# Gate products with the gate-scaled one-hot as the stationary operand and the plain one-hot streamed

## The chip, the core and the metric

The kernel runs as one program on one core of a Trainium2 chip. Its engines are TensorE (PE; PEld is its weight load), VectorE (DVE), ScalarE (ACT), GpSimd (POOL) and SyncE (SP, which here only issues transfers). The metric is the device time of one execution in microseconds; lower is better. The kernel before takes 2062.15 us, the median of three runs (2058.58 to 2062.66).

## What is computed

Two decoder layers over 256 tokens of 1024 channels, in float32. Each has a mixer (layer 0: mLSTM heads beside block-sparse attention; layer 1: differential attention) and then a PEER channel mixer, which is where the change lies. PEER looks up 128 of 16384 experts for each token: 8 heads, 16 experts each. The reference, cut to that:

```
qry = (xt @ wq).reshape(t, 8, 2, 128)
sub = einsum('thpd,pnd->thpn', qry, keys)            # 2 x 128 sub-keys
s_top, i_top = top_k(sub, 16)
cand_s = s_top[:, :, 0, :, None] + s_top[:, :, 1, None, :]
cand_i = i_top[:, :, 0, :, None] * 128 + i_top[:, :, 1, None, :]
score, pos = top_k(cand_s, 16); idx = cand_i at pos
gate = softmax(score)
act = gelu(einsum('td,thkd->thk', xb, u[idx])) * gate
out = einsum('thk,thkd->td', act, v[idx])
```

An expert's number is 128 i + j, with i from the first half of the keys and j from the second.

## The kernel before

The kernel gathers nothing. It computes all 16384 activations for all 256 tokens, multiplies them by a gate that is zero nearly everywhere, and multiplies by all of v. Products stand in float32 precision by two parts: every weight tile of 128x1024 is loaded by SP (`load`, L149) into a ring, copied by ScalarE to a rounded part hi (L159), and VectorE forms the rest lo (L162). TensorE then runs three products for each of the eight channel blocks (L185 hi by hi, L186, L187), each with 128x128 stationary weights and 256 moving tokens.

PEER (`peer_body`) has four stages for each layer:

- 16 query tiles and the scores; VectorE starts on the top-16 searches.
- The first tiles of u (`h_tile`, one tile of 128 experts, all j of one i): A[:, i, :] = gelu(u_i . h), while VectorE finishes the searches. They leave three tables with the 128 slots (16 x 8 heads) on partitions and the tokens along the free axis: "i" and "g" (the gate, scaled by 32768, in two fp16 parts) and "jn", the negative of j.
- The gate stretch: the other tiles of u up to 128, and between them 64 gate groups of four tokens each (`G_TOK`), spread evenly up to tile 120. Most tiles have a group behind them, about every fourth has none.
- 128 tiles of v (L920 to L922), with A as the activations.

The gate of token t for expert (i, j) is the sum over the slots k of g_k (j_k = j)(i_k = i). That is a product of two one-hot matrices over the 128 slots. `gate_onehots` makes them for four tokens: oj, the one-hot of j, a dense block of 128 values of j for each token (by ScalarE with five activations in five of eight groups, L1068 and L1069, else by VectorE, L1072); oi, the one-hot of i with the four tokens innermost (VectorE, L1078), and og, that times either part of the gate (L1081, twice). `gate_group` then runs eight products (L1094: four tokens by two parts) with 128 slots as the contraction, oj as the stationary operand and og[:, w, :, k] as the moving one; they add up in PSUM to [j, 4 tokens, i]. Below the tile at which the stretch stands, VectorE multiplies A by them (L1101); above, ScalarE writes them into A (L1103), and a later `h_tile` multiplies by gelu (L950).

The order is that of the Python code, per engine, after a scheduler that may move an instruction on its own engine. The one-hots of group n + 1 are asked for ahead of the products of group n. og and the dense one-hot have two buffers, the plain token-innermost one has one; PSUM tiles "h" and "g" have two banks each. On TensorE a group stands whole between the 24 products of one tile and those of the next.

Of the kernel before, what the change touches and what calls it, by code (L numbers as in the profile page):

```python
# [20 lines left out]
P = 128  # L21
# [34 lines left out]
class Cols:  # L56
    """Column offsets of the packed per-partition constants."""
# [17 lines left out]
class Prog:  # L75
# [8 lines left out]
    # ---------------------------------------------------------------- setup  # L84
# [52 lines left out]
    def psum(self, tag):  # L137
        """One PSUM bank: h, g in every phase; l, t in the mixers and acc in the PEER."""
        pool, bufs = (self.ps, 2) if tag in "hg" else (self.ps2, {"l": 2, "t": 2, "acc": 4}[tag])
        return pool.tile([P, 512], F32, tag=tag, name=f"ps_{tag}", bufs=bufs)  # L140
# [4 lines left out]
    # ------------------------------------------------------------- weights  # L145
# [6 lines left out]
    def split(self, raw, late=None):  # L152
        """A tile as the sum of two that products take in one pass; from late on, the parts are left to norm_apply."""
# [20 lines left out]
    def mm_col(self, pss, ws, act, kds=range(KD)):  # L174
        """pss[i][128, 256] = ws[i]^T @ act over 1024 rows; both operands in two parts."""
# [13 lines left out]
    def col_tiles(self, aps, act, tags, kds=range(KD), ws=None, rest=None):  # L189
        """Products of the first few tiles, channel block by channel block as act's blocks come in; then one by one."""  # L190
# [11 lines left out]
    def take(self, ap):  # L202
        """The split tile of ap; the splits of the tiles that follow in self.feed go out ahead of need."""
        if not self.feed and not self.ready:
            return self.wsplit(ap)
        while self.feed and len(self.ready) <= AHEAD:
            self.ready.append(self.wsplit(self.feed.pop(0)))
        return self.ready.pop(0)

    def first_tiles(self, aps, late):  # L210
        """The first three tiles of a phase, loaded into the ring that outlives the phases."""
# [14 lines left out]
    def mm_row(self, pss, aps, act):  # L226
        """pss[tt][128 tokens, 512] = act^T @ w, w in four tiles of 2 x 128 rows."""
# [15 lines left out]
    # --------------------------------------------------------------- adaLN  # L243
    def ada(self, layer, cb, kds=range(KD)):
        """mod columns of block cb: (silu(c) @ ada_w + ada_b), channels on partitions."""
# [13 lines left out]
    # ---------------------------------------------------------------- norms  # L259
    def rsqrt(self, out, v):  # L260
        """out = v ** -0.5 for positive v, elementwise on a small tile."""
        self.nc.gpsimd.tensor_tensor(out=out, in0=v, in1=self.mhalf[:, :v.shape[-1]], op=ALU.pow)

    def keep_warm(self, n):
        """Products without a use while the norm's short chain runs: an idle tensor engine halves its clock."""
# [5 lines left out]
    def norm_stat(self, kd, warm=WARM):  # L271
        """Adds the squares of channel block kd; after the last, sums over channels, tokens on partitions."""
# [37 lines left out]
    def norm_apply(self, layer, which, r, t, hhi, hlo, kds=range(KD)):  # L310
        """h = x * rstd * (gain (1 + scale)) + shift in two parts; t holds the unshifted blocks."""
# [19 lines left out]
    def alibi(self, pool):  # L331
        """Distances from a query to the keys before it, without bound for the keys behind it."""
# [12 lines left out]
    # ------------------------------------------------- attention primitives  # L345
# [8 lines left out]
    def qk_norm(self, pool, zs):  # L354
        """RMS norm over each 64 channels of a q tile and a k tile; q also takes the logits' scale."""
# [29 lines left out]
    def softmax(self, pool, lg, q, k, h, qt, bias):  # L385
        """exp(logits - max) and its sum; q [64, 256], k [64, 256] of one head."""
# [12 lines left out]
    def transpose_p(self, pool, p0, p1):  # L399
        """P of both query tiles -> [keys 0..127, 256 queries], [keys 128..255, queries 128..255]."""  # L400
# [17 lines left out]
    # ------------------------------------------------------------- mixer 0  # L418
# [105 lines left out]
    def moba_pair(self, pool, hp, zs, bv, bias, yhi, ylo):  # L524
        """One pair of heads, in stages."""
# [32 lines left out]
    def advance(queue):  # L558
        """Takes each head in flight one stage further, the oldest first."""
# [4 lines left out]
    def mlstm_gates(self, pool, gp, out):  # L564
        """Row quantities of the mLSTM, one head per partition, time along the free axis."""
# [39 lines left out]
    def mlstm(self, pool, rows, qk, mv, mo, yhi, ylo):  # L605
# [12 lines left out]
        # state after the first chunk, its normaliser as column 128  # L618
# [21 lines left out]
        # num and, as column 128, den, tokens on partitions  # L640
# [34 lines left out]
        # h = num / max(|den|, exp(-m)); rms_norm(h) folds into one factor per token  # L675
# [30 lines left out]
    # ------------------------------------------------------------- mixer 1  # L706
    def mixer1(self):
# [3 lines left out]
        with ExitStack() as st:  # L711
# [28 lines left out]
            for i, ps in self.col_tiles(cols, h, ("h", "h", "l"), ws=ws):  # L740
# [6 lines left out]
                if i == 3:  # L747
                    # lambda, on every partition
# [18 lines left out]
    def diff_head(self, pool, hd, zs, v, vhave, bias, lam, og, yhi, ylo):  # L767
        """One head, in stages."""
# [44 lines left out]
    # ---------------------------------------------------------------- PEER  # L813
# [5 lines left out]
    def peer_body(self, layer, side, st):  # L819
# [7 lines left out]
        tabs = {"i": tab.tile([P, T], F16, name="it"), "jn": tab.tile([P, T], F32, name="jn"),  # L827
# [103 lines left out]
    def ffn_out(self, layer, kd, y):  # L931
        """x += gate * y for one block of channels."""
# [8 lines left out]
    def h_tile(self, ap, h, A, i, done=0):  # L941
        """A[:, i, :] = gelu(u_i . h), times the gates of the tokens below done, which A holds."""
# [11 lines left out]
    def scores(self, pool, subs, q, keys):  # L954
        """Products of one half head's queries with its sub-keys, tokens on partitions."""
# [24 lines left out]
    def top_k(self, sp, vals, idxs, tabs):  # L980
        """Top 16 of the 16 x 16 sums per head: expert rows i, columns j and gates, slots on partitions."""
# [8 lines left out]
        for tt in range(TT):  # L990
# [15 lines left out]
            # softmax gates  # L1006
# [10 lines left out]
            # position -> (a, b): 4 x 16 candidates, then 12 x 4  # L1017
# [13 lines left out]
            # b = (pos & 3) + (pos < 64) * (pos & 12),  pos & 3 = pos - 4 * (pos >> 2)  # L1031
# [23 lines left out]
            nc.vector.tensor_copy(tabs["i"][:, t], ps[:, 0:P])  # L1055
            nc.vector.tensor_scalar_mul(tabs["jn"][:, t], ps[:, P:2 * P], -1.0)
# [146 lines left out]
```

## Time and profile before

| what | value |
|---|---|
| median of the runs | 2062.15 us |
| span of the profiled execution | 2059.4 us (the page gives no other time for it) |
| TensorE busy | 2020.4 us, 98% |
| VectorE busy | 1536.9 us, 75% |
| ScalarE busy | 1136.4 us, 55% |
| moved by DMA | 376.84 MB, 183 GB/s on average |
| gate products (L1094) | 1024, 138.8 us busy with overlap |

Times in the rows are microseconds unless marked ns. A busy TensorE says little by itself: products overlap in the record, so one that follows another at 0.12 us has a duration of 0.28 us. What a product costs is read from start to start. PE and PEld rows count the same 16281 products and their loads.

### The profile page before, as it was taken

The numbers are of one execution on the slowest core, as the hardware profiler recorded it, in microseconds if no ns is written. First come the engines' busy times: TensorE is split into PE (matmuls) and PEld (weight loads), VectorE is DVE, ScalarE is ACT, GpSimd is POOL, SyncE is SP. The second block draws the span as 40 slices with busy tenths as digits, with TensorE's granted clock in tenths as the row PEclk, the third lists the DMA queues.
The fourth block names the chain that finished last, engine by engine and source line by source line (L and its number), as shares of the span: only waits on it lengthen the run. The fifth ranks groups of instructions, "written<-read, shape, count | busy, mean of one in ns | idle before, by whom it ended". The sixth has DMA issues, their size and how long they took to land.

```text
span 2059.4 us, 41035 instructions
## 1 busy us (share of the span) xinstructions
PE 2020.4 (98%) x16281; PEld 1963.3 (95%) x16281; DVE 1536.9 (75%) x3328; ACT 1136.4 (55%) x2129; POOL 48.3 (2%) x37
## 2 busy tenths in 40 slices
PE   5999999999999999999999999999999999999999
PEld 4888999999999999999988799999999999999999
DVE  8978998787897565677578789977788965556654
ACT  4655546777665444444455654667767644444443
POOL 0010000000000000000022100000000000000000
PEclk9999999999999999999999999999999999999999
DMA  8863355444444566898266143544444455559660
GB/s 329 293 192 131 114 185 177 144 152 146 142 152 159 200 211 202 329 321 301 91 226 204 52 159 121 185 165 152 145 146 150 145 167 183 184 186 343 217 192 25
DMA packets 104016, 376.84 MB, mean 183 GB/s; under 512 B 11536, under 2 KB 12944, under 8 KB 103696
## 3 DMA queue, kind: packets, MB, share of 16 engines
q1 hardware_dynamic: 103824, 374.22, 53.6%
q8 instruction: 128, 2.10, 0.4%
q14 instruction: 64, 0.52, 0.1%
HBM read 373.12 MB, written 1.05 MB: 182 GB/s over the span
## 4 chain that ended last, share of the span: by engine, by line
PE 88%; issue 5%; DVE 5%; ACT 1%; POOL 1%; DMA 0%; POOLq 0%; ACTq 0%; DVEq 0%
PE ps_h L185 13%; PE ps_h L187 13%; PE ps_h L186 13%; PE ps_acc L921 9%; PE ps_acc L922 9%; PE ps_acc L920 9%; PE ps_g L1094 6%; PE ps_h L922 3%; PE ps_h L921 3%; PE ps_h L920 3%; DVE lo L162 1%; PE ps_l L389 1%; PE ps_h L237 1%; PE ps_h L238 1%; PE ps_h L239 1%
## 5 line engine op out<-in xcount | busy, mean ns | idle before, releaser
L159 ACT CAST hi<-raw 128x1024 fp32r<-128x1024 f32 x613 | 640.6, 1046 | 730.6 <-PE ps_h L921 385.9
L162 DVE TENSOR_TENSOR lo<-raw,hi 128x1024 fp32r<-128x1024 f32 x613 | 748.7, 1221 | 346.4 <-ACT hi L159 342.8
L185 PE MATMUL ps_h<-h2hi,hi 128*128 128x256 f32 x2256 | 653.0, 289 | 0.4 <-ACT A L952 0.4
L186 PE MATMUL ps_h<-h2lo,hi 128*128 128x256 f32 x2256 | 638.4, 283 | 0.0
L187 PE MATMUL ps_h<-h2hi,lo 128*128 128x256 f32 x2256 | 638.2, 283 | 0.0
L185 PEld LDWEIGHTS ps_h<-h2hi,hi 128*128 128x128 f32 x2256 | 434.2, 192 | 1.2 <-ACT A L952 0.9
L920 PE MATMUL ps_acc<-act,hi 128*128 128x256 f32 x1536 | 434.4, 283 | 0.7 <-ACT act L904 0.7
L921 PE MATMUL ps_acc<-act,hi 128*128 128x256 f32 x1536 | 434.4, 283 | 0.1
L922 PE MATMUL ps_acc<-act,lo 128*128 128x256 f32 x1536 | 433.9, 283 | 0.0
L186 PEld LDWEIGHTS ps_h<-h2lo,hi 128*128 128x128 f32 x2256 | 433.0, 192 | 0.0
L187 PEld LDWEIGHTS ps_h<-h2hi,lo 128*128 128x128 f32 x2256 | 432.2, 192 | 0.7
L920 PEld LDWEIGHTS ps_acc<-act,hi 128*128 128x128 f32 x1536 | 294.5, 192 | 2.0 <-ACT act L904 1.7
L921 PEld LDWEIGHTS ps_acc<-act,hi 128*128 128x128 f32 x1536 | 294.8, 192 | 0.5 <-DVE act L905 0.5
L922 PEld LDWEIGHTS ps_acc<-act,lo 128*128 128x128 f32 x1536 | 294.7, 192 | 0.0
L1101 DVE SCALAR_TENSOR_TENSOR A<-A,ps_g 128x256 f32<-128x256 f32 (+28 forms) x214 | 124.5, 582 | 45.1 <-PE ps_g L1094 41.8
L921 PE MATMUL ps_h<-act,hi 128*128 128x256 f32 x512 | 144.8, 283 | 0.0
L922 PE MATMUL ps_h<-act,lo 128*128 128x256 f32 x512 | 144.8, 283 | 0.0
L920 PE MATMUL ps_h<-act,hi 128*128 128x256 f32 x512 | 144.6, 283 | 0.0
L1094 PE MATMUL ps_g<-og,oj 128*128 128x128 f16 x1024 | 138.8, 292 | 0.0
L252 DVE CUSTOM_DVE_ANT_0 raw<-raw,crow,small 128x1024 f32<-128x1024 f32 x96 | 122.6, 1279 | 18.3 <-DMA raw<-in_ada_w_dram 18.0
L1103 ACT ACTIVATE A<-ps_g 128x256 f32<-128x256 f32 (+39 forms) x170 | 69.4, 447 | 95.7 <-DVE A L1101 90.2
L1081 DVE TENSOR_TENSOR og<-oi,gt 128x512 f16<-128x512 f16 x256 | 100.9, 420 | 25.2 <-PE ps_g L1094 25.2
(319 smaller groups left out, 2654.7 us busy)
## 6 DMA issues: line engine op xcount, KB each, us to landing
raw<-in_uT_dram SPq DMA_DIRECT2D x256, 512.0 KB, 3.3
raw<-in_v_dram SPq DMA_DIRECT2D x256, 512.0 KB, 4.3
raw<-in_ada_w_dram SPq DMA_DIRECT2D x96, 512.0 KB, 4.6
raw<-in_wq_dram SPq DMA_DIRECT2D x32, 512.0 KB, 4.4
raw<-in_ev_in_dram SPq DMA_DIRECT2D x21, 512.0 KB, 5.1
raw<-in_od_in_dram SPq DMA_DIRECT2D x16, 512.0 KB, 4.4
raw<-in_ev_v_dram SPq DMA_DIRECT2D x8, 512.0 KB, 4.8
raw<-in_ev_out_dram SPq DMA_DIRECT2D x8, 512.0 KB, 4.1
```

Source lines behind the costliest of these rows:

```text
L159: nc.scalar.copy(hi, raw)
L162: self.last_lo = nc.vector.tensor_tensor(out=lo, in0=raw, in1=hi.bitcast(F32), op=ALU.subtract)
L185: nc.tensor.matmul(ps, lhsT=whi[:, s], rhs=ahi[:, kd, :], start=kd == kds[0], stop=False)
L186: nc.tensor.matmul(ps, lhsT=whi[:, s], rhs=alo[:, kd, :], start=False, stop=False)
L187: nc.tensor.matmul(ps, lhsT=wlo[:, s], rhs=ahi[:, kd, :], start=False, stop=kd == kds[-1])
L252: nc.vector.tensor_tensor_reduce(w, w, self.crow, 1.0, self.small[:, ab:ab + 1], ALU.mult, ALU.add, m)
L920: nc.tensor.matmul(acc[dt], lhsT=vhi[:, s], rhs=xhi, start=False, stop=False)
L921: nc.tensor.matmul(acc[dt], lhsT=vhi[:, s], rhs=xlo, start=False, stop=False)
L922: nc.tensor.matmul(acc[dt], lhsT=vlo[:, s], rhs=xhi, start=False, stop=m == NEXP - 1 and dt not in (0, 2))
L1081: nc.vector.tensor_tensor(out=og[:, w], in0=oi, in1=tabs["g"][:, w, ts].unsqueeze(1).to_broadcast(full), op=ALU.mult)
L1094: nc.tensor.matmul(pv[:, k, :], lhsT=oj[:, k, :], rhs=og[:, w, :, k], start=w == 0, stop=w == 1)
L1101: nc.vector.scalar_tensor_tensor(dst, dst, 1.0 / GSC, pv[:, :, lo:m], op0=ALU.mult, op1=ALU.mult)
```

## The change

The roles of the two one-hots are exchanged. The token-innermost one, which carries the gates, now stands for j (oj and og), and og[:, w, :, k] becomes the stationary operand. The dense plain one stands for i (oi) and is the moving operand. The output in PSUM is the same [j, token, i]. The tables follow: "in" is the negative of i in float32, "j" is j in fp16. Cut to the core:

```
-        tabs = {"i": tab.tile([P, T], F16, name="it"), "jn": tab.tile([P, T], F32, name="jn"),
+        tabs = {"in": tab.tile([P, T], F32, name="in"), "j": tab.tile([P, T], F16, name="jt"),
                 "g": tab.tile([P, 2, T], F16, name="gt")}
...
-            nc.vector.tensor_copy(tabs["i"][:, t], ps[:, 0:P])
-            nc.vector.tensor_scalar_mul(tabs["jn"][:, t], ps[:, P:2 * P], -1.0)
+            nc.vector.tensor_scalar_mul(tabs["in"][:, t], ps[:, 0:P], -1.0)
+            nc.vector.tensor_copy(tabs["j"][:, t], ps[:, P:2 * P])
...
     def gate_onehots(self, oh, tabs, t0):
         nc = self.nc
         ts = slice(t0, t0 + G_TOK)
-        oj = oh.tile([P, G_TOK, P], F16, tag="oj", name="oj")
+        oi = oh.tile([P, G_TOK, P], F16, tag="oi", name="oi")
         if self.ngate % 8 < J_ACT:
             for k in range(G_TOK):
-                nc.scalar.activation(oj[:, k, :], self.iota, AF.Square, bias=tabs["jn"][:, t0 + k:t0 + k + 1])
-            nc.scalar.activation(oj, oj, AF.Relu, scale=-1.0, bias=1.0)
+                nc.scalar.activation(oi[:, k, :], self.iota, AF.Square, bias=tabs["in"][:, t0 + k:t0 + k + 1])
+            nc.scalar.activation(oi, oi, AF.Relu, scale=-1.0, bias=1.0)
         else:
             for k in range(G_TOK):
-                nc.vector.tensor_scalar(oj[:, k, :], self.iota, tabs["jn"][:, t0 + k:t0 + k + 1], 0.0, op0=ALU.add,
+                nc.vector.tensor_scalar(oi[:, k, :], self.iota, tabs["in"][:, t0 + k:t0 + k + 1], 0.0, op0=ALU.add,
                                         op1=ALU.is_equal)
         self.ngate += 1
-        oi = oh.tile([P, NEXP, G_TOK], F16, tag="oi", name="oi", bufs=1)
-        og = oh.tile([P, 2, NEXP, G_TOK], F16, tag="og", name="og")
-        full = [P, NEXP, G_TOK]
-        nc.vector.tensor_tensor(out=oi, in0=self.iota4, in1=tabs["i"][:, ts].unsqueeze(1).to_broadcast(full),
+        oj = oh.tile([P, P, G_TOK], F16, tag="oj", name="oj", bufs=1)
+        og = oh.tile([P, 2, P, G_TOK], F16, tag="og", name="og")
+        full = [P, P, G_TOK]
+        nc.vector.tensor_tensor(out=oj, in0=self.iota4, in1=tabs["j"][:, ts].unsqueeze(1).to_broadcast(full),
                                 op=ALU.is_equal)
         for w in range(2):
-            nc.vector.tensor_tensor(out=og[:, w], in0=oi, in1=tabs["g"][:, w, ts].unsqueeze(1).to_broadcast(full),
+            nc.vector.tensor_tensor(out=og[:, w], in0=oj, in1=tabs["g"][:, w, ts].unsqueeze(1).to_broadcast(full),
                                     op=ALU.mult)
-        return oj, og
+        return oi, og
 
     def gate_group(self, ohs, A, t0, i_mul):
         nc = self.nc
         ts = slice(t0, t0 + G_TOK)
-        oj, og = ohs
+        oi, og = ohs
         pv = self.psum("g").rearrange("p (t i) -> p t i", t=G_TOK)
         for k in range(G_TOK):
             for w in range(2):
-                nc.tensor.matmul(pv[:, k, :], lhsT=oj[:, k, :], rhs=og[:, w, :, k], start=w == 0, stop=w == 1)
+                nc.tensor.matmul(pv[:, k, :], lhsT=og[:, w, :, k], rhs=oi[:, k, :], start=w == 0, stop=w == 1)
```

On TensorE, at the first gate groups of layer 0, these are the rows before, each load above its product (semaphores that a row waits for in brackets):

```order
L187 MATMUL ps_h<-h2hi,lo 128x256
L1094 LDWEIGHTS oj [waits DVE_49,Activation_49]
L1094 MATMUL ps_g<-og,oj 128x128 [waits PE_49]
L1094 LDWEIGHTS oj
L1094 MATMUL ps_g<-og,oj 128x128 [waits DVE_49]
L1094 LDWEIGHTS oj
L1094 MATMUL ps_g<-og,oj 128x128
```

And the same place now, where oi is the plain one-hot and og the one with the gates:

```order
L187 MATMUL ps_h<-h2hi,lo 128x256
L1094 LDWEIGHTS og [waits PE_49,DVE_49]
L1094 MATMUL ps_g<-oi,og 128x128 [waits Activation_49]
L1094 LDWEIGHTS og [waits DVE_49]
L1094 MATMUL ps_g<-oi,og 128x128
L1094 LDWEIGHTS og
L1094 MATMUL ps_g<-oi,og 128x128
```

No row moved; the loads now read og and wait for VectorE, which makes it, and the products read the plain one-hot. Before, the two products of a token had the same weights; now each has its own.

On VectorE, the piece of the difference at the first gate groups of layer 0 (A is named by its number, it and jt are the fp16 tables):

```order
-L1081 TENSOR_TENSOR og<-oi,gt 128x512 x2
+L1081 TENSOR_TENSOR og<-oj,gt 128x512 x2
 L162 TENSOR_TENSOR lo<-raw,hi 128x1024
 L1101 SCALAR_TENSOR_TENSOR A_2063<-A_2063,ps_g 128x4x38
-L1078 TENSOR_TENSOR oi<-iota_91,it 128x512
-L1081 TENSOR_TENSOR og<-oi,gt 128x512 x2
+L1078 TENSOR_TENSOR oj<-iota_91,jt 128x512
+L1081 TENSOR_TENSOR og<-oj,gt 128x512 x2
 L950 TENSOR_TENSOR A_2063<-A_2063,gelu 128x4
 L162 TENSOR_TENSOR lo<-raw,hi 128x1024
```

The shapes and the order are the same as before; only the names of the operands differ.

## Rows read from the trace of the kernel before

**Rows 1.** The page, its span, two engines, and the granted clock in 40 slices.

```profile
span 2059.4 us, 41035 instructions
...
PE 2020.4 (98%) x16281; PEld 1963.3 (95%) x16281; DVE 1536.9 (75%) x3328; ACT 1136.4 (55%) x2129; POOL 48.3 (2%) x37
...
PEclk9999999999999999999999999999999999999999
...
GB/s 329 293 192 131 114 185 177 144 152 146 142 152 159 200 211 202 329 321 301 91 226 204 52 159 121 185 165 152 145 146 150 145 167 183 184 186 343 217 192 25
```

**Rows 2.** The page, the chain that ended last: shares of the span by line.

```profile
PE ps_h L185 13%; PE ps_h L187 13%; PE ps_h L186 13%; PE ps_acc L921 9%; PE ps_acc L922 9%; PE ps_acc L920 9%; PE ps_g L1094 6%; PE ps_h L922 3%; PE ps_h L921 3%; PE ps_h L920 3%; DVE lo L162 1%; PE ps_l L389 1%; PE ps_h L237 1%; PE ps_h L238 1%; PE ps_h L239 1%
```

**Rows 3.** Timeline of TensorE around one gate group: start, us, engine, line, operands, count.

```profile
606.97 0.28 PE L187 MATMUL ps_h<-h2hi,lo 128*128 128x256 f32 x1
607.09 1.08 PE L1094 MATMUL ps_g<-og,oj 128*128 128x128 f16 x8
607.93 0.37 PE L185 MATMUL ps_h<-h2hi,hi 128*128 128x256 f32 x1
608.13 0.28 PE L186 MATMUL ps_h<-h2lo,hi 128*128 128x256 f32 x1
```

**Rows 4.** All instructions of line 1094: duration ns min/median/max, first and last start us.

```profile
L1094 PEld LDWEIGHTS <-oj x1024: 96/115/118, 355.8 to 1658.5; 128*128 128x128 f16 x171
L1094 PE MATMUL ps_g<-og,oj x1024: 274/294/296, 355.8 to 1658.7; 128*128 128x128 f16 x171
```

**Rows 5.** Float32 weight loads of 4, 64 and 128 columns: lines 372, 551, 363.

```profile
L372 PEld LDWEIGHTS ps_g<-ident,qr x24: 81/83/85, 104.8 to 1154.7; 128*4 128x4 f32 x24
...
L551 PEld LDWEIGHTS ps_t<-pT,bv x16: 137/137/137, 141.0 to 164.6; 128*64 128x64 f32 x16
...
L363 PEld LDWEIGHTS ps_g<-ind,qsq x96: 186/192/224, 94.8 to 1147.7; 128*128 128x128 f32 x96
```

**Rows 6.** All instructions of line 268, products of dense fp16 columns without a use.

```profile
L268 PEld LDWEIGHTS <-zero x24: 95/97/181, 185.1 to 1198.8; 128*128 128x128 f16 x24
L268 PE MATMUL ps_h<-iota,zero x24: 376/379/392, 185.2 to 1199.0; 128*128 128x512 f16 x24
```

**Rows 7.** Timeline of TensorE where three of line 268 follow each other.

```profile
185.15 0.82 PE L268 MATMUL ps_h<-iota,zero 128*128 128x512 f16 x3
```

**Rows 8.** Timeline of the weight loads of four products with two moving columns.

```profile
94.78 0.52 PEld L363 LDWEIGHTS ps_g<-ind,qsq 128*128 128x128 f32 x4
```

**Rows 9.** Gate stage stretches: length, PE, PEld, DVE, ACT, POOL busy, clock, DMA, GB/s.

```profile
355.00:400.00 45.00, 45.00 (x381) 44.52 (x380) 32.74 (x77) 35.48 (x91) 0.00 (x0) 1.00 0.42 142
...
600.00:640.00 40.00, 40.00 (x338) 39.60 (x338) 37.64 (x80) 26.18 (x67) 0.00 (x0) 1.00 0.45 147
```

**Rows 10.** Timeline of VectorE late in layer 0, one round with a gate group.

```profile
626.29 0.75 DVE L1101 SCALAR_TENSOR_TENSOR A<-A,ps_g 128x256 f32<-128x256 f32 x1 [1.07 <-PE ps_g L1094]
626.96 0.41 DVE L1081 TENSOR_TENSOR og<-oi,gt 128x512 f16<-128x512 f16 x1
627.29 0.39 DVE L950 TENSOR_TENSOR A<-A,gelu 128x232 f32<-128x232 f32 x1
627.60 0.58 DVE L1101 SCALAR_TENSOR_TENSOR A<-A,ps_g 128x196 f32<-128x196 f32 x1
628.10 0.41 DVE L1081 TENSOR_TENSOR og<-oi,gt 128x512 f16<-128x512 f16 x1
628.43 1.21 DVE L162 TENSOR_TENSOR lo<-raw,hi 128x1024 fp32r<-128x1024 f32 x1
629.57 0.41 DVE L1078 TENSOR_TENSOR oi<-iota,it 128x512 f16<-128x512 f16 x1
```

**Rows 11.** All instructions of line 1072, VectorE's way to the dense one-hot.

```profile
L1072 DVE TENSOR_SCALAR oj<-iota,jn x192: 235/252/292, 368.8 to 1653.4; 128x128 f16<-128x128 f16 x192
```

**Rows 12.** Waits in layer 0's gate stage: who waited for whom, us, times, longest.

```profile
DVE A L1101 <- PE ps_g L1094: 19.7, 28, 1.4
DVE og L1081 <- PE ps_g L1094: 12.6, 12, 1.5
```

## Prediction

> **What bounds the kernel now.** I read the page first: the span is 2059.4 us, TensorE is busy for 98% of it, and its granted clock stands at 9 tenths or more, which is its upper level of 2.4 GHz, in all 40 slices [rows 1]. So the clock is no lever, and what counts is how TensorE's time is filled. The chain of waits comes next: six entries for the big products, and at 6% the gate products of line 1094 [rows 2]. Nothing of VectorE but a few splits is on it. So an edit of the gate products changes the span one for one, as long as no other engine takes over.
>
> The timeline of TensorE shows what a gate group costs [rows 3]. From the start of L187 at 606.97 to the start of L186 at 608.13 are 1.16 us, with a group of eight between. Products of one tile follow at 0.12 us, so L187 to the L186 behind it is 0.24 us without a group. The group costs 0.92 us, 115 ns for each product. There are 1024 products [rows 4], so 128 groups and 118 us, close to the chain's 6% (124 us, rounded).
>
> What sets the 115 ns? A product has a load of 128 stationary columns and a stream of 128 moving ones. The load: float32 loads last 83 ns for 4 columns, 137 for 64 and 192 for 128 [rows 5], so about 80 ns that all have and 0.87 ns for a column. The fp16 load of the gate product lasts 96 ns when nothing holds it up (its minimum; 118 at most) [rows 4]. That leaves some 16 ns for the columns themselves, far less than 115. The stream: the products without a use of line 268 move 512 fp16 columns that lie densely. Three of them take 0.82 us with 0.38 for the last [rows 6, 7], so they follow at 0.22 us, 55 ns for 128 columns. Their duration says it again: at 0.43 ns a column, 384 columns fewer would shorten 379 ns to 214, and the gate product's shortest is 274 [rows 4, 6], 60 ns more. Its moving operand is og[:, w, :, k], every fourth fp16. So I read the 115 ns as a stream at half rate (110) and 5 ns of turnover; the load is hidden.
>
> **The change, part by part.** The number, shape and type of all instructions stay. The two one-hots trade places: the moving one (oi) is now dense, and the stationary one (og) is read with a step of four elements.
>
> *The stream.* 128 dense columns at line 268's rate take 55 ns instead of 110. This is the term on which all rests.
>
> *The load.* No row shows a strided stationary operand. From below: it costs what the dense fp16 load costs, 16 ns behind the fixed part, hidden behind 55 ns of stream; the pace is then 55 plus the 5 of turnover, 60 ns. From above: it falls back to the float32 load's pace, which is (0.52 - 0.19) / 3 = 110 ns where only two columns are streamed [rows 8], or even takes twice that, as the stream does now (220). I take the doubling of the fast load, 16 to 32 ns, since the same step doubles the stream; that still fits behind 55, and I leave 5 ns more for it in the open: 65 ns. The Trainium skill says in "TensorE: Matmul & The Clock Gate" (Weight-path perf modes) that the fast load applies to 128 weights that are not FP32, in four chunks packed or strided. By that the slow bound would not arise; the 96 ns against 192 agree on the type, and no run here shows the step. The same page (Back-to-back issue gap) gives about 81 ns as the sustained pace of load and product at 128 columns; as an estimate from it, a group would take 7 x 81 + 110 = 677 ns, save 243, and the time would be some 31 us under before's.
>
> *The last product of a group.* Behind it the float32 weights of L185 must be loaded, 110 ns, and only 65 ns of stream stand before them. So the eighth slot stays at 110. The group takes 7 x 65 + 110 = 565 ns instead of 920; it saves 355 ns, and 128 groups save 45 us.
>
> *VectorE and ScalarE.* Their instructions only trade operands: the table that is negated is now that of i, a 128x128 copy against a 128x128 scaling, twice per layer: nothing. But they have less time. In the gate stretches TensorE waits for nobody; VectorE is busy for 32.7 of 45 us early and 37.6 of 40 late [rows 9], because the part of A that it multiplies grows. Late in the layer, a round with a group takes 0.75 + 0.41 + 0.39 + 0.58 + 0.41 + 1.21 + 0.41 = 4.16 us of VectorE durations [rows 10]; neighbours overlap by some 0.08 us, so 3.6 us, and in 3 of 8 groups VectorE also makes the dense one-hot, four times 0.25 us [rows 11], 0.7 net of overlap. A round on TensorE shrinks from 3.80 to 2.88 + 0.57 = 3.45 us, but every fourth tile has no group, which gives VectorE its slack: over four tiles TensorE needs 4 x 2.88 + 3 x 0.565 = 13.2 us and VectorE about 3 x 3.6 + 1.6 + 0.8 = 13.2. So it is even only at the end of each layer, in the last 40 us or so of 285; before, VectorE has room. Its waits for the gate products (19.7 and 12.6 us in layer 0) [rows 12] are slack that it gives up first. I charge 3 us for both layers together; between 0 and 15 is possible. ScalarE has 26 to 35 us of work in 40 to 45 [rows 9]: covered. The weights arrive at 142 to 147 GB/s there [rows 9] and would have to come 9% faster; the first twentieth of the span moves twice that [rows 1].
>
> **Sum.** 2059.4 - 45 + 3 = 2017 us by the profiled span. The page gives no other time for that execution; the median of the runs shown, 2062.15, is 2.7 above, and I add 2.
>
> **Rivals.**
> *The load is half hidden.* The strided load steals reads from the stream or is turned over later, pace 80 to 105. A group then takes 670 to 845 ns and saves 250 to 75: 32 to 10 us, 2030 to 2052. For it: load and stream of a product both read SBUF, and the step has never been measured here. Against: float32 loads of 110 ns hide behind 120 ns products throughout.
> *VectorE becomes the bound.* If it cannot be filled beyond the 94% of the late windows [rows 9], the last 90 of 285 us of a layer shrink not at all: a third of the gain goes, 45 x 2/3 = 30, so 2032. Against: where VectorE idles late, it mostly waits for the gate product itself [rows 12].
> *Nothing changes.* Either the strided load falls to 110 ns, so 8 x 110 = 880 ns a group and 5 us won, or something else than the stream paces the products at 115, and the time stays at 2062. In this kernel the second would be a turnover per product that doesn't depend on the operands' step. Against it: pairs with float32 weights turn over at 110 ns [rows 8], so 115 is no floor of a pair. The Trainium skill, "SBUF — State Buffer" (Door 1: The DMA port swizzle), has a rule that speaks for it: access is at full rate as long as two elements fall into one 16-byte line, so up to 8 bf16 apart. By that rule a step of four is free now and there is nothing to win in the stream; the 60 ns that the gate product is too long speak against it.
> *Slower.* The strided stationary operand loses the fast path and pays double for the step as well: 220 ns, which nothing hides. A group then takes 8 x 220 = 1760 ns, 840 more: +107 us, 2169. It decides from a load of 115 ns on; at 130 it would be +15 us. For it: the stream pays just that today. Against: the load would have to become more than seven times as long as its 16 ns.
>
> **How the numbers follow.** Forecast (pace 55 to 80) 0.62; VectorE bound 0.12; half hidden 0.10; nothing changes 0.09; slower 0.07. The predicted time is 2019 us. Its own range is 2008 to 2032: the low end is a pace of 60 with nothing lost to VectorE (7 x 60 + 110 = 530, 390 saved, 50 us) and a little more. The range with the rivals goes up to 2050, which leaves out the last two cases and a few hundredths below. Faster by over 0.2% (about 4 us, what can be told from no change) 0.84, within 0.09, slower 0.07.
>
> **What would show it.** The start of L187 to that of L186 across a group should fall from 1.16 to about 0.81 us; the 128 groups should leave the chain with some 3 to 4% instead of 6. The fp16 load should show about 110 ns unhindered, not 190: that is the step on which I could be wrong. TensorE should stay without idle time in the gate stretches until their last 40 us, where a wait of L187 for the split of line 162, or of the gate product for og, may appear. I am wrong if the pace stays at 110 or more, or if TensorE's idle time takes back over 15 us.

## The result, and the profile after

The kernel after the change takes 2011.34 us (median of four runs, 2009.66 to 2012.62), against 2061.49 us for four runs of the kernel before (2058.58 to 2062.66): a ratio of 0.9756, 95% interval 0.9743 to 0.977. The forecast was 2019 us with a range of 2008 to 2050. The direction and the mechanism came out as argued; the gain is 50 us where 43 were forecast.

The page after, with the lines that answer to [rows 1, 2], and two of its groups (instructions, then busy us, mean ns of one, idle time of the engine before them and what ended it):

```profile
span 2010.8 us, 41035 instructions
...
PE 1970.7 (98%) x16281; PEld 1912.6 (95%) x16281; DVE 1536.1 (76%) x3328; ACT 1131.6 (56%) x2129; POOL 48.3 (2%) x37
...
PEclk9999999999999999999999999999999999999999
...
PE ps_h L185 14%; PE ps_h L187 14%; PE ps_h L186 14%; PE ps_acc L921 9%; PE ps_acc L922 9%; PE ps_acc L920 9%; PE ps_g L1094 3%; PE ps_h L922 3%; PE ps_h L921 3%; PE ps_h L920 3%; PE ps_l L389 1%; DVE lo L162 1%; DVE raw L252 1%; PE ps_acc L959 1%; DMA raw<-in_ev_in_dram 1%
...
L1101 DVE SCALAR_TENSOR_TENSOR A<-A,ps_g 128x256 f32<-128x256 f32 (+28 forms) x214 | 124.2, 581 | 11.9 <-PE ps_g L1094 11.0
...
L1081 DVE TENSOR_TENSOR og<-oj,gt 128x512 f16<-128x512 f16 x256 | 100.6, 419 | 13.3 <-PE ps_g L1094 13.1
```

The number of instructions, the clock and TensorE's busy share are those of before. One entry of the chain moved by more than a point: line 1094 falls from 6 to 3%. In microseconds the span lost 48.6, and VectorE's work stayed at 1536 us. The group lines show where slack went: VectorE now stands idle for 11.9 us ahead of its multiplications L1101 and for 13.3 ahead of L1081. In the kernel before, the same two lines of the page read 45.1 and 25.2 us:

```profile
L1101 DVE SCALAR_TENSOR_TENSOR A<-A,ps_g 128x256 f32<-128x256 f32 (+28 forms) x214 | 124.5, 582 | 45.1 <-PE ps_g L1094 41.8
...
L1081 DVE TENSOR_TENSOR og<-oi,gt 128x512 f16<-128x512 f16 x256 | 100.9, 420 | 25.2 <-PE ps_g L1094 25.2
```

The timeline of TensorE around one gate group after (start, us, engine, line, operands, count), as in [rows 3]:

```profile
606.43 0.28 PE L187 MATMUL ps_h<-h2hi,lo 128*128 128x256 f32 x1
606.56 0.64 PE L1094 MATMUL ps_g<-oi,og 128*128 128x128 f16 x8
607.00 0.36 PE L185 MATMUL ps_h<-h2hi,hi 128*128 128x256 f32 x1
607.21 0.28 PE L186 MATMUL ps_h<-h2lo,hi 128*128 128x256 f32 x1
```

From the start of L187 to that of L186 are 0.78 us, of which 0.24 are the products of the tile: the group costs 0.54 us, where it cost 0.92 [rows 3]. By the ends of the products, over all 128 groups, the medians are 534 ns after and 929 before. So 395 ns are saved, and 128 times that is 50.5 us.

The weight loads beside it, in the same view (PEld rows):

```profile
606.32 0.19 PEld L187 LDWEIGHTS ps_h<-h2hi,lo 128*128 128x128 f32 x1
606.55 0.48 PEld L1094 LDWEIGHTS <-og 128*128 128x128 f16 x8
606.98 0.19 PEld L185 LDWEIGHTS ps_h<-h2hi,hi 128*128 128x128 f32 x1
```

and all instructions of line 1094 after (duration ns min/median/max, first and last start), as in [rows 4]:

```profile
L1094 PEld LDWEIGHTS <-og x1024: 112/114/137, 356.6 to 1609.7; 128*128 128x128 f16 x171
L1094 PE MATMUL ps_g<-oi,og x1024: 219/219/248, 356.6 to 1609.7; 128*128 128x128 f16 x171
```

The product's record is 55 ns shorter than the shortest of before (219 against 274), as much as half of the 110 ns of stream that the prediction read. The strided load lasts 112 ns at its shortest, 16 more than the dense one. The first load of the group starts 0.23 us behind that of L187, where float32 loads follow each other at 0.12: a late start that the prediction did not see. It was there to be seen. In the kernel before, the first load of a group starts as late (235 ns in all 128 groups of both kernels):

```profile
606.85 0.19 PEld L187 LDWEIGHTS ps_h<-h2hi,lo 128*128 128x128 f32 x1
607.09 0.80 PEld L1094 LDWEIGHTS <-oj 128*128 128x128 f16 x8
```

But there the first product ended 117 ns behind the float32 product, hardly more than the 116 between the others: the slow stream hid the late load.

Two stretches after, the gate stage of layer 0 (first to last group) and a late part of it (length, then PE, PEld, DVE, ACT, POOL busy with counts, clock, DMA share, GB/s), to be held against [rows 9]:

```profile
356.60:623.50 266.90, 266.90 (x2458) 264.19 (x2457) 241.21 (x545) 203.36 (x515) 0.00 (x0) 1.00 0.48 159
580.00:615.00 35.00, 35.00 (x323) 34.66 (x322) 34.60 (x77) 25.19 (x66) 0.00 (x0) 1.00 0.49 161
```

The same stage before, less 0.3 us at its ends, in the same view:

```profile
356.00:648.00 292.00, 292.00 (x2457) 289.19 (x2456) 242.66 (x547) 206.35 (x517) 0.00 (x0) 1.00 0.44 147
```

From the start of its first gate product to the end of its last, the stage takes 267.1 us instead of 292.3, so it is 25.2 us shorter, in layer 1 as well, and TensorE is busy for all of it. The weights came at 159 instead of 147 GB/s. The v tiles take 369.7 us per layer in both kernels. That makes 50.4 us of the two gate stages; the span lost 48.6, and the 1.8 between lie outside these stages. That is within what two runs of one kernel differ by: in a second profile of the kernel after (after_again), the first gate stage starts 2.5 us earlier.

### The profile page after: what moved, and what is told of

It is laid out like the page before. It is cut to its first block, busy times and chain, and to the rows that moved or that the text cites. A ratio compares the mean times of both kernels' runs of the same rounds, so it can differ in the third digit from the quotient of the medians.

```text
span 2010.8 us, 41035 instructions
## 1 busy us (share of the span) xinstructions
PE 1970.7 (98%) x16281; PEld 1912.6 (95%) x16281; DVE 1536.1 (76%) x3328; ACT 1131.6 (56%) x2129; POOL 48.3 (2%) x37
## 4 chain that ended last, share of the span: by engine, by line
PE 88%; issue 6%; DVE 3%; DMA 2%; ACT 1%; POOL 1%; POOLq 0%; ACTq 0%; DVEq 0%; SPq 0%
PE ps_h L185 14%; PE ps_h L187 14%; PE ps_h L186 14%; PE ps_acc L921 9%; PE ps_acc L922 9%; PE ps_acc L920 9%; PE ps_g L1094 3%; PE ps_h L922 3%; PE ps_h L921 3%; PE ps_h L920 3%; PE ps_l L389 1%; DVE lo L162 1%; DVE raw L252 1%; PE ps_acc L959 1%; DMA raw<-in_ev_in_dram 1%
## 5 line engine op out<-in xcount | busy, mean ns | idle before, releaser
L185 PE MATMUL ps_h<-h2hi,hi 128*128 128x256 f32 x2256 | 652.9, 289 | 0.5
L187 PE MATMUL ps_h<-h2hi,lo 128*128 128x256 f32 x2256 | 638.3, 283 | 0.0
L186 PE MATMUL ps_h<-h2lo,hi 128*128 128x256 f32 x2256 | 638.3, 283 | 0.0
L185 PEld LDWEIGHTS ps_h<-h2hi,hi 128*128 128x128 f32 x2256 | 432.0, 191 | 1.9 <-ACT A L952 1.0
L186 PEld LDWEIGHTS ps_h<-h2lo,hi 128*128 128x128 f32 x2256 | 433.0, 192 | 0.0
L187 PEld LDWEIGHTS ps_h<-h2hi,lo 128*128 128x128 f32 x2256 | 432.3, 192 | 0.7
L1101 DVE SCALAR_TENSOR_TENSOR A<-A,ps_g 128x256 f32<-128x256 f32 (+28 forms) x214 | 124.2, 581 | 11.9 <-PE ps_g L1094 11.0
L1081 DVE TENSOR_TENSOR og<-oj,gt 128x512 f16<-128x512 f16 x256 | 100.6, 419 | 13.3 <-PE ps_g L1094 13.1
L1068 ACT ACTIVATE oi<-iota,in 128x128 f16<-128x128 f16 x320 | 107.1, 394 | 0.0
```

Of the source, the lines that this page charges most:

```text
L185: nc.tensor.matmul(ps, lhsT=whi[:, s], rhs=ahi[:, kd, :], start=kd == kds[0], stop=False)
L186: nc.tensor.matmul(ps, lhsT=whi[:, s], rhs=alo[:, kd, :], start=False, stop=False)
L187: nc.tensor.matmul(ps, lhsT=wlo[:, s], rhs=ahi[:, kd, :], start=False, stop=kd == kds[-1])
L1068: nc.scalar.activation(oi[:, k, :], self.iota, AF.Square, bias=tabs["in"][:, t0 + k:t0 + k + 1])
L1081: nc.vector.tensor_tensor(out=og[:, w], in0=oj, in1=tabs["g"][:, w, ts].unsqueeze(1).to_broadcast(full), op=ALU.mult)
L1101: nc.vector.scalar_tensor_tensor(dst, dst, 1.0 / GSC, pv[:, :, lo:m], op0=ALU.mult, op1=ALU.mult)
```

## The experiments

All line numbers below are those of the kernel in question. "Pace" is the mean time from the end of one gate product to the next inside a group, "entry" the time from the end of the last float32 product to that of the first gate product, "exit" the time from the end of the last gate product to that of L185. They are medians over the groups, worked out from the records; the rows shown are samples. An undisturbed float32 product ends 120 ns behind the one before it.

**e1_move_steps: the step of the moving operand, by itself.** The kernel before with its roles; the group's number modulo 4 chooses a step of 1, 2, 4 or 8 fp16 elements for the moving operand.

```
+        flat = og.rearrange("p w i t -> p (w i t)")
+        every = lambda s: flat[:, :128 * s].rearrange("p (a s) -> p a s", s=s)[:, :, 0]
+        case = t0 // G_TOK % 4
...
-                nc.tensor.matmul(pv[:, k, :], lhsT=oj[:, k, :], rhs=og[:, w, :, k], ...)
+                nc.tensor.matmul(pv[:, k, :], lhsT=oj[:, k, :], rhs=every(S), ...)   # S = 1, 2, 4, 8: L1099, 1101, 1103, 1105
```

> The kernel before (stationary one-hot dense), but the moving operand of the eight products is read with a step of 1, 2, 4 or 8 fp16 values, by turns from group to group; the gates are then not the reference's. Theory (the step of the moving operand sets the pace): 55 to 60 ns a product at step 1; the same at step 2, since the big products stream 4 bytes a column at full rate; 115 at step 4 as before; 115 to 220 at step 8. Rival (something else than the step paced the products, such as two products with the same weights in a row): about 115 at all four. Rival by the Trainium skill, SBUF - State Buffer, two elements in a 16-byte line suffice: about 55 at 1, 2 and 4, more at 8. Span: with 32 groups at each step, two thirds of a microsecond a group saved on 64 groups, about 2030 us by the theory.

TensorE at one group of each step, 1, 2, 4 and 8 in turn (start, us, line, count):

```profile
356.46 0.62 PE L1099 MATMUL ps_g<-og,oj 128*128 128x128 f16 x8
356.89 0.36 PE L185 MATMUL ps_h<-h2hi,hi 128*128 128x256 f32 x1
...
359.84 0.64 PE L1101 MATMUL ps_g<-og,oj 128*128 128x128 f16 x8
360.29 0.36 PE L185 MATMUL ps_h<-h2hi,hi 128*128 128x256 f32 x1
...
363.24 1.08 PE L1103 MATMUL ps_g<-og,oj 128*128 128x128 f16 x8
364.08 0.37 PE L185 MATMUL ps_h<-h2hi,hi 128*128 128x256 f32 x1
...
367.04 1.98 PE L1105 MATMUL ps_g<-og,oj 128*128 128x128 f16 x8
368.65 0.48 PE L185 MATMUL ps_h<-h2hi,hi 128*128 128x256 f32 x1
```

From the first gate product to L185 are 0.43, 0.45, 0.84 and 1.61 us. The pace is 55.9, 58.0, 115.9 and 227 ns, a whole group 513, 531, 929 and 1817 ns, and the dense load stays at 95 to 96 ns at its shortest throughout. So the step of the moving operand alone sets the pace: two elements are nearly free, and at four and at eight the time doubles with the step. Step eight lies a little over the 220 ns that I expected at most. The rival that two products with the same weights are slow for another reason falls, because the pairs of equal weights are here too and run at 56 ns with a dense stream. The rule of the Trainium skill that the prediction weighed ("SBUF — State Buffer", Door 1: The DMA port swizzle), full rate up to 8 bf16 apart, holds here for a step of two and fails at four (115.9 ns) and eight (227 ns); the measurement decides. The time was 2066.79 us in one run (before 2059.96, median of 13). My expectation of a span near 2030 was wrong by its own sum: the slow groups of step 8 (888 ns over a group of before) eat what the dense ones (416 less) and those of step 2 (398 less) give; with 32 groups each that is 2.4 us more, not 30 less. The two gate stages grew by 1.25 us each, just that; the rest of the measured difference lies outside them.

**e2_load_steps: the step of the stationary operand, by itself.** The kernel after, with oi streamed densely, and the same four steps for the stationary operand.

```
-                nc.tensor.matmul(pv[:, k, :], lhsT=og[:, w, :, k], rhs=oi[:, k, :], ...)
+                nc.tensor.matmul(pv[:, k, :], lhsT=every(S), rhs=oi[:, k, :], ...)   # S = 1, 2, 4, 8: L1099, 1101, 1103, 1105
```

> The changed kernel (moving one-hot dense), but the stationary operand is read with a step of 1, 2, 4 or 8 fp16 values by turns; the gates are not the reference's. Theory (the step lengthens the load, which stays hidden behind the stream): shortest load 96 ns at step 1, 96 to 104 at 2, 112 at 4, 112 to 145 at 8; pace 56 ns a product at 1, 2 and 4; a group 16 ns cheaper at step 1 than at 4, because the first load of a group shows. At 8 either 56 still or, if its load costs over 55 ns behind the fixed 80, more. Rival (the step of the stationary operand costs nothing at all): the same load, pace and group at every step.

The loads of the four steps (duration ns min/median/max):

```profile
L1099 PEld LDWEIGHTS <-og x256: 96/98/99, 355.5 to 1597.4; 128*128 128x128 f16 x128
...
L1101 PEld LDWEIGHTS <-og x256: 96/98/100, 358.8 to 1603.6; 128*128 128x128 f16 x128
...
L1103 PEld LDWEIGHTS <-og x256: 111/113/130, 362.2 to 1607.0; 128*128 128x128 f16 x128
...
L1105 PEld LDWEIGHTS <-og x256: 142/148/167, 365.6 to 1610.5; 128*128 128x128 f16 x128
```

Take off 80 ns, the part that float32 loads have whatever their columns [rows 5], and the columns cost 16, 16, 31 and 62 ns: the same pattern as the stream's, free at two, doubled at four and again at eight. That fp16 loads have the same fixed part is an estimate, not measured by itself; the doubling fits it. The pace is 55.9, 55.9, 55.9 and 62.4 ns. So inside a group a load shows in the pace only when its column part (62) is longer than the stream (56), and the 80 ns stay hidden. Float32 weights fit that too: 192 less 80 is 112, and their pairs turn over at 110 [rows 8]. By the Trainium skill ("TensorE: Matmul & The Clock Gate", Weight-path perf modes) the fast load holds for packed and for strided weights; the trace agrees so far that even at eight the load, 148 ns in the median, stays under the float32 load's 192 ns. The group takes 513, 513, 531 and 607 ns, so the step of four costs 18 ns a group, 16 of them at the entry. There the load is in the open: the first load of a group lasts 96, 96, 112 and 142 ns, and the entry is 73, 73, 89 and 119 ns, longer by the same amounts. One run took 2013.3 us.

**e3_both_strided: the new load with the old stream.** The kernel after, og[:, w, :, k] on both sides.

```
-                nc.tensor.matmul(pv[:, k, :], lhsT=og[:, w, :, k], rhs=oi[:, k, :], ...)
+                nc.tensor.matmul(pv[:, k, :], lhsT=og[:, w, :, k], rhs=og[:, w, :, k], ...)
```

> The changed kernel, but the moving operand is og with its step of four again, so both operands are strided; the gates are not the reference's. Only the stream part of the change is undone. Theory (the dense stream is the whole gain): 115 ns a product, a group 920 to 950 ns, 2058 to 2066 us, as the kernel before. Rival (it is the exchange of roles, the stationary operand that carries the gates, that brought it): 56 ns a product and 2011 us. Between them only if two strided operands disturb each other: over 120 ns a product and over 2066 us.

One group on TensorE:

```profile
355.05 0.28 PE L187 MATMUL ps_h<-h2hi,lo 128*128 128x256 f32 x1
355.17 1.11 PE L1094 MATMUL ps_g<-og 128*128 128x128 f16 x8
356.03 0.37 PE L185 MATMUL ps_h<-h2hi,hi 128*128 128x256 f32 x1
356.24 0.29 PE L186 MATMUL ps_h<-h2lo,hi 128*128 128x256 f32 x1
```

L187 to L186 is 1.19 us again, a group 953 ns at a pace of 117.4. Ten runs gave 2064.25 us (2061.98 to 2067.65), a ratio of 1.0022 (1.0013 to 1.0032). With the moving operand strided as before, the exchange gives nothing and costs some 4 us; 24 ns more a group are 3 of them. The dense stream is the whole gain.

**e4_const_operands: loads that wait for no one-hot.** The kernel after, with the constants iota4 and iota as operands of the gate products, to see whether the late first load is a wait for og.

```
-                nc.tensor.matmul(pv[:, k, :], lhsT=og[:, w, :, k], rhs=oi[:, k, :], ...)
+                nc.tensor.matmul(pv[:, k, :], lhsT=self.iota4[:, :, k], rhs=self.iota, ...)
```

> The changed kernel, but the gate products read two constants (stationary with a step of four, moving dense), so that their loads wait for no one-hot; the gates are not the reference's. It asks why the first product of a group ends 91 ns after the product before it instead of 56. Theory (an fp16 load behind a float32 product starts late whatever it waits for): still 85 to 95 ns, a group 530 ns, span as the changed kernel's, 2005 to 2012. Rival (the semaphore wait on the first load keeps it from being pulled ahead): the first product ends 55 to 65 ns after, a group takes 500 ns, span 3 to 5 us shorter.

The loads at one group:

```profile
361.59 0.19 PEld L187 LDWEIGHTS ps_h<-h2hi,lo 128*128 128x128 f32 x1
361.82 0.48 PEld L1094 LDWEIGHTS <-iota 128*128 128x128 f16 x8
362.25 0.19 PEld L185 LDWEIGHTS ps_h<-h2hi,hi 128*128 128x128 f32 x1
```

The first fp16 load still comes 0.23 us behind the last float32 load, the entry is 90 ns and the exit 174. In 110 of the 128 groups that load now waits for no semaphore at all, and it starts 234 to 236 ns late in every one. So the delay is not a wait for the one-hots. It goes with the change from float32 to fp16 operands: in the kernel after, four fp16 loads of line 891 behind L187 also start 235 ns later, while ten float32 loads for the same PSUM tile "g" (lines 1050 and 1052) start 136 or 137 ns behind L187. What in the engine makes it was not tried. The time, 2030.2 us in one run against an expected span of 2005 to 2012, missed: each gate stage grew by some 8 us. TensorE's order is the same, but without the one-hots' dependences the instructions of VectorE and ScalarE came out in another order, and TensorE now waits for ScalarE, which waits for VectorE. The waits of this gate stage in layer 0 (us, times, longest):

```profile
ACT A L1103 <- DVE A L1101: 61.2, 38, 3.8
...
PEld ps_h L185 <- ACT A L952: 7.3, 13, 1.1
PE ps_h L185 <- ACT A L952: 4.6, 10, 0.9
```

So this kernel answers the question on the load and says nothing on the time.

**e5_pairs: half as many changes between float32 and fp16.** If 35 ns are in the open at the entry and 53 at the exit, two groups back to back save 88 ns. The products of two groups are issued together, then their uses.

```
...
-                nxt = self.gate_onehots(oh, tabs, done + G_TOK) if done + G_TOK < T else None
-                self.gate_group(ohs, A, done, i)
-                ohs = nxt
-                done += G_TOK
+                pvs = [self.gate_mm(o) for o in ohs]
+                for pv in pvs:
+                    self.gate_use(pv, A, done, i)
+                    done += G_TOK
+                ohs = pair(done) if done < T else None
```

> The changed kernel with the gate groups in pairs: sixteen products in a row after about every third tile, then the uses, then the one-hots of the next pair. Same result. A group in the changed kernel takes 531 ns: 8 x 56 = 446, some 35 before its first product and 53 behind its last, where float32 weights must be loaded. Theory (those 85 to 90 ns are paid once for each change between fp16 and float32 products): 64 of 128 are saved, 5.5 us, 2005 to 2007 us. Rival (the one-hots of the next pair, which now can only be made after this pair's products, come late, or VectorE's bursts delay the splits of the weights): TensorE waits, 2009 to 2020 us.

One pair on TensorE:

```profile
354.76 0.28 PE L187 MATMUL ps_h<-h2hi,lo 128*128 128x256 f32 x1
354.88 1.08 PE L1093 MATMUL ps_g<-oi,og 128*128 128x128 f16 x16
355.77 0.36 PE L185 MATMUL ps_h<-h2hi,hi 128*128 128x256 f32 x1
355.97 0.28 PE L186 MATMUL ps_h<-h2lo,hi 128*128 128x256 f32 x1
```

L187 to L186 is 1.21 us, so a pair costs 0.97 (median 980 ns by the ends) and two groups apart 2 x 534 = 1068: the 88 ns are real, 5.6 us over 64 pairs. But the time is 2011.71 us (2010.23 to 2011.97; ratio 0.9765, 0.9752 to 0.9778), no better than the change alone. Waits of TensorE in the first gate stage (those of its products alone; its loads wait for the same three):

```profile
PE ps_h L185 <- ACT A L954: 1.0, 3, 0.4
PE ps_h L187 <- DVE lo L162: 1.0, 1, 1.0
PE ps_g L1093 <- DVE og L1083: 0.3, 1, 0.3
```

To count the loss, take every step from one product's end to the next that is over 200 ns, less the 120 of an undisturbed one: 4.49 us in that stage and 2.75 in the second, 7.2 together, where the change alone has none. A reading that fits, not shown by itself: twice the one-hots and twice the multiplications of A now come at once, and the weight splits and ScalarE's copies stand behind them.

**e6_jact2 and e7_jact8: is VectorE the next bound?** The kernel after with one number changed: ScalarE makes the dense one-hot in two of eight groups, or in all, instead of five.

```
-J_ACT = 5
+J_ACT = 2      # e6; 8 in e7
```

> The changed kernel with the dense one-hot on ScalarE in 2 of 8 groups instead of 5; VectorE gets 24 more per layer, about 17 us of work in a gate stage of 267 us in which it is 92% busy. Same result. Theory (VectorE just holds pace in the changed kernel and has no room left late in the stage): TensorE waits, each gate stage 4 to 12 us longer, 2020 to 2035 us. Rival (VectorE's busy share overstates its need): the stages stay at 267 us and the time within 2 us of the changed kernel's.

> The changed kernel with the dense one-hot on ScalarE in all groups; VectorE loses about 17 us of work per layer. Same result. Theory (TensorE never waits in the gate stage of the changed kernel, so relieving VectorE brings nothing): stages of 267 us, time within 2 us of 2011. Rival (VectorE holds TensorE back somewhere): 1 to 4 us shorter. ScalarE could become late instead, at some 90% busy: up to 5 us longer.

The late stretch of e7, to be held against the one shown of after:

```profile
580.00:615.00 35.00, 35.00 (x323) 34.66 (x322) 32.87 (x61) 30.05 (x80) 0.00 (x0) 1.00 0.47 160
```

VectorE has 1.7 us less to do in these 35, and TensorE does exactly the same: the gate stages are 267.1 us, as after, without a lost step. One run took 2009.26 us; what it is below the change alone lies ahead of the first gate stage, which starts 3 us earlier in this execution. With more work on VectorE (e6) the stages are 268.3 us; by the count of steps over 200 ns, 1.37 and 1.35 us are lost, all within the last 21 us of each stage. That is far less than the 4 to 12 us that I expected (and VectorE's busy share after is 90%, 241.2 of 266.9 us, not 92). So VectorE is not a bound after the change and comes within a few microseconds of being one at the end of each layer. The single run of e6 took 2019.34 us; some 8 us over the change alone, of which the gate stages and what stands right behind them make about 5. The rest lies in the mixer of layer 1, where two profiles of the change itself differ by 2 us, and is not explained.

**e8_pairs_spread and e9_pairs_jact7: pairs, with the work around them spread.** In e8 the products of two groups go together, but behind each tile only one group's use and one group's one-hots are issued. e9 is the same with the dense one-hot on ScalarE in seven of eight groups.

```
...
+                if not held and issued < T and (i == NEXP or issued < T * (i - i_start) / (I_STOP - i_start)):
+                    held = [self.gate_mm(o) for o in ohs]
+                    issued, ohs = issued + 2 * G_TOK, []
+                if held:
+                    self.gate_use(held.pop(0), A, done, i)
+                    done += G_TOK
+                    if made < T:
+                        ohs.append(self.gate_onehots(oh, tabs, made))
+                        made += G_TOK
...
-J_ACT = 5
+J_ACT = 7      # e9 only
```

> Gate groups in pairs as in the run before, but their uses and the next one-hots are spread over the two tiles behind the pair, one group's share for each tile, so that VectorE gets no burst. Same result. In the run with plain pairs a pair cost 980 ns instead of twice 534, as forecast, but TensorE then waited 4.5 and 2.7 us in the two gate stages. Theory (those waits came from the bursts): stages of 264 us without waits, 2005 to 2007 us. Rival (the waits come with the pairs however the uses are placed, since both PSUM banks and both one-hot buffers are held at once): 2010 to 2013 us.

> The same with the dense one-hot on ScalarE in 7 of 8 groups instead of 5. Same result. If what waits remain are VectorE's, they go: 2005 to 2007 us. Rival (ScalarE, which must also copy the weights, becomes the late one): over 2008 us.

> The changed kernel once more, on the same chip as the two versions with pairs, to compare with them: 2009 to 2013 us, gate stages of 266.9 us.

Waits in the gate stage of layer 0, those of ScalarE for VectorE's multiplications of A and those of TensorE's products, first e8:

```profile
ACT A L1113 <- DVE A L1111: 35.1, 28, 2.8
...
PE ps_g L1099 <- ACT A L1113: 1.3, 2, 0.8
...
PE ps_g L1099 <- ACT gelu L957: 0.5, 1, 0.5
...
PE ps_g L1099 <- DVE oj L1086: 0.2, 1, 0.2
```

and e9:

```profile
ACT A L1113 <- DVE A L1111: 16.9, 17, 2.4
...
PE ps_g L1099 <- ACT gelu L957: 0.4, 1, 0.4
```

e8 took 2010.88 us (2009.53 to 2013.16; ratio 0.9756, 0.9742 to 0.977): its lost steps, 3.06 and 2.48 us by the same count, are again as large as the 5.6 gained. So my theory missed: spreading the work does not take the waits away, and the time is in the range of the rival. By the rows, TensorE now waits for ScalarE's writes into A, and these wait for VectorE's multiplications of A. With fewer one-hots on VectorE, in e9, ScalarE waits half as long and TensorE loses 0.67 us per stage; the time is 2007.54 us (2005.71 to 2008.90; ratio 0.9738, 0.9724 to 0.9752), a little over the 2005 to 2007 that I expected. So with pairs VectorE's work does hold TensorE back, where it did not with single groups (e7). The change itself, run beside them five times more, took 2011.64 (2010.06 to 2013.51; ratio 0.9756, 0.9742 to 0.9771). e9 is 4.1 us below it and the two sets of runs don't overlap; 2 x (2.8 - 0.67) = 4.3 us is what the pairs should give. The other part of the edit gives nothing without the pairs: in e7, with all dense one-hots on ScalarE, the gate stages did not change. e9 beats both kernels.

## Why the prediction was right, point by point

- *The stream* (55 ns dense against 110): right. The pace is 55.9 ns against 115.9, and e1 and e3 show that nothing else is needed for it.
- *The load* (the doubling of 16 to 32 ns taken, between 16 and 110): right, and e2 shows the doubling by itself, 31 ns. The choice between the ends rested on the likeness to the stream, and the likeness holds from step two to step eight. The pace did not hang on it: by e2 anything up to the stream's 56 ns would have been hidden.
- *The pace of 65:* mis-sized. Neither the 5 ns of turnover nor the 5 ns of load "in the open" show; it is 55.9. Over seven products this is 64 ns a group, 8 us in all.
- *The last slot of 110:* right. L185 ends 173 ns behind the last gate product instead of the usual 120, so 53 are in the open behind 56 of stream: 109.
- *The first slot:* missed. The first product ends 91 ns behind the float32 product instead of 56, 35 more, since its load comes late and, with the step, lasts some 16 ns longer. The error offsets about half of the one in the pace, which is luck: the group came out nearer to the forecast than either term. Edge to edge the group is 91 + 7 x 55.9 + 173 + 120 - 240 = 535 ns; the prediction had 565.
- *VectorE* (3 us charged): nothing was lost. The balance of 13.2 against 13.2 us over four tiles was right in that VectorE is busy for 34.60 of 35 us, and wrong in what follows from it: no step of TensorE in the gate stages is lost. VectorE's work has slack to be shifted within the stage, and in e6 it took over the dense one-hots of three more groups in eight for 1.2 us a stage.
- *The sum:* the profiled span is 2010.8 us against 2017 forecast. Of the 6 us between them, 5 are the groups (50.5 saved, 45 forecast: 8 for the pace, less 4 to 5 for the first slot, and 1 because a group of before costs 929 ns by the medians and not 920), 3 are VectorE's charge, and nearly 2 go the other way outside the stages.
- *The rivals:* the half-hidden load and the slower case fall by e2 (the load would have to go beyond step eight to matter much); the floor per product falls by e1; VectorE as the bound falls by e7, for single groups.

## What to carry to other kernels

Where one operand of a product must be strided, let it be the stationary one as long as its load, less the fixed part that overlaps, is shorter than the stream; the moving operand paid in full for the steps of four and eight fp16 elements measured here. Price a short group of products by three numbers read from end to end, the entry, the pace and the exit, since with a pace of 56 ns the two edges are a sixth of the group. Look for the edges in the kernel before, too: the late load stood there, hidden. A neighbour engine that is busy for 99% of a stretch need not be a bound; a run with less work on it tells. Here such a run changed nothing with single groups, and did with pairs.

## What the runs showed of the hardware

- A stream of 128 fp16 columns takes 55.9, 58.0, 115.9 and 227 ns at steps of 1, 2, 4 and 8 elements; a load of 128 fp16 columns takes 96, 96, 111 and 142 ns at its shortest. Other types and longer steps were not run.
- Loads and products overlap so that inside a group a pair takes the longer of the stream and the load's column part (62.4 ns at step eight, 55.9 below). The sustained 81 ns at 128 columns that the Trainium skill gives ("TensorE: Matmul & The Clock Gate", Back-to-back issue gap) was not met: runs of 8 and of 16 pairs, each with a load of its own, went at 55.9 ns.
- A change from float32 products to fp16 ones and back costs 35 + 53 = 88 ns beside the products themselves (16 of the 35 are the stationary operand's step of four), and it was saved in full where two groups went together (980 ns for 1068). The fp16 load behind a float32 one starts 235 ns after it, with or without a wait for a semaphore; a float32 one that nothing holds up, behind L187, 120 to 137.
